# A hybrid encoder layer in fp32r: seven weight slots handed out from one free pool instead of in turn

## The chip, the cores and the metric

The kernel runs on one core of a Trainium2 chip. The metric is the device time of one launch in microseconds, the median over several runs; the profile is one further execution of the same program, recorded by the hardware profiler.

## The reference

One inference step of a layer with two branches, on a prompt of 1024 tokens and a sample of 32 tokens with a cache of 128 keys (model width 1024, 8 heads, DFF 2816). Cut to what matters:

```
mod  = silu(c) @ w_ada + b_ada                      # six shift/scale/gate vectors
h    = rms_norm(x) * (1 + scale1) + shift1
q, k, v, xin, gb, gc, ga_br, gb_br = split(h @ w_in)
o    = rms_norm(softmax(q1 k1) v - lam * softmax(q2 k2) v)   # chunk-causal, 8 heads, q/k normed
y_a  = o @ w_attn_out
y_b  = (gb * short_conv(gc * xin)) @ w_conv_out     # width 3, per channel
x    = x + gate1 * ((sigmoid(ga_br) * y_a + sigmoid(gb_br) * y_b) @ w_out)
h2   = rms_norm(x) * (1 + scale2) + shift2
g, up = split(h2 @ w_gate_up)
x    = x + gate2 * ((silu(g) * up) @ w_down)
```

## The kernel before, in words

**Precision.** Every product is computed from operands split into a high part (fp32r) and a low part (the remainder): `split` is a cast on ScalarE (L84) and a subtraction on VectorE, or on GpSimd where the caller says so (L85). Each product takes three matmuls, high times high, high times low, low times high.

**Dense stages by Strassen.** The 1056 token columns are four quarters of 264. The conv inputs (sections 3 and 5 of `w_in`), the branch gates (sections 6 and 7) and gate_up multiply a pair of 128-wide weight columns at a time: `wstrassen` loads the two columns (`kt_stage`, L108, into two staging buffers with the tag "st"), takes their four blocks A11, A12, A21, A22, forms S1 to S4 from them in place in the staging buffers (L150 S3, L152 S1, L155 S2, L160 S4) and splits seven tiles, in the order A11, A22, S2, S1, A12, S3, S4 (S4's low part on GpSimd). S2 is made from A22, S4 from A12 and S2. `strassen` multiplies in the order of `SEQ`: A11, S2, S1, A12, S3, S4, A22. Each of the seven products is 12 matmuls (L184) for each of two halves of the tokens, so a set is 168 matmuls of 264 columns. Sums and activations leave PSUM through L188 to L201; eight PSUM tiles a set come from a pool of six.

```
SEQ = (("A11", "B11", "X"), ("S2", "T2", "Y"), ("S1", "T1", "Z"), ("A12", "B21", "X"),
       ("S3", "T3", "V"), ("S4", "B22", "Z"), ("A22", "T4", "V"))
```

The conv stage has eight sets in turns (xin, then gc; after each gc set the convolution L506/L508 on VectorE), the gate stage eight sets with two `ada_step`s after each (chains of L360 on VectorE that compute the adaLN vectors, closed by small transposes on TensorE, L367), gate_up 22 sets.

**Dense stages without Strassen.** conv_out, attn_out and out split a weight column into two tiles (`wpiece`), the down projection into three for each half of DFF (`d_piece`); they use the tiles in the order in which they make them.

**Attention.** `run_plan` fixes the order of TensorE, ScalarE, VectorE and GpSimd from estimated times: 72 units (8 heads, 9 token tiles), each a generator per engine. `act_thread` writes the exponentials p (L882) into tiles of the weight slots: the planner counts five of them (`R["p"]`, a ring). `filler` computes the section gb of the projection (L1050 to L1052) wherever TensorE is free, from two further slots (`wf`, cast at L1036, low part at L1038), eight times.

**Slots.** The pool `W` holds the two staging buffers and seven weight slots of 4 KB a partition. `w_slot` gives out the tags ws0 to ws6 in turn, each with one buffer: tile number i always has the slot of tile i - 7. Also the first adaLN weights (`ada_load`) take their places so. In attention p has ws0 to ws4 in turn and `wf` ws5 and ws6. A tile's first write waits until all reads of the tile before it in its slot are done.

**Order of the work.** TensorE's instructions run in program order. Outside attention, the order of ScalarE, VectorE, GpSimd and SP (which issues the DMAs) is set by the compiler's scheduler, which takes the instruction that is first in the program among those whose operands and slots it estimates to be ready. On the chip each engine then keeps that order.

Of the kernel before, what the change touches and what calls it, by code (L numbers as in the profile page):

```python
# [7 lines left out]
F32 = mybir.dt.float32  # L8
F32R = mybir.dt.float32r
# [5 lines left out]
P = 128  # L15
D = 1024
KT = 8
# [17 lines left out]
def f(ap):  # L35
    return ap.bitcast(F32)


def hybrid_layer(tc, x_prompt, x_sample, cache_k, cache_v, state_conv, c_prompt, c_sample,
# [8 lines left out]
    def sb(name, bufs=1, side="left"):  # L48
        return tc.alloc_tile_pool(name=name, bufs=bufs, side=side, reuse_waits="tile")
# [17 lines left out]
    W = sb("W")  # L67
# [16 lines left out]
        act.copy(hi, src)  # L84
        (lo_eng or dve).tensor_sub(lo, src, f(hi))  # L85

    wsn = [0]

    def w_slot(shape, dtype, name):

        wsn[0] += 1
        return W.tile(shape, dtype, tag=f"ws{wsn[0] % 7}", name=name, bufs=1)

    def ws_tile():

# [532 lines left out]
    def run_plan():  # L628
        while threads:
# [10 lines left out]
            try:  # L640
# [5 lines left out]
    R = {k: Ring(n) for k, n in (("qd", 4), ("kraw", 3), ("kd", 3), ("QK", 2), ("p", 5), ("aT0", 2), ("aT1", 1), ("o", 2),  # L646
                                 ("on", 2), ("sq", 1), ("cv", 2))}
# [22 lines left out]
    def head_tiles(h):  # L670
        if h not in heads:
            K = A.tile([P, 8, 2, P], F32R, tag="K", name="K", bufs=2)
            Ks = A.tile([P, 2, P + DS], F32R, tag="Ks", name="Ks", bufs=2)
            V = A.tile([P, 10, VD], F32, tag="V", name="V", bufs=2)
            ck = A.tile([P, 2, HD], F32, tag="ck", name="ck", bufs=1)
            sp.dma_start(ck, cache_k[0, 0, :, h])
            sp.dma_start(V[:, 8, :], cache_v[0, 0, :, h])
            heads[h] = K, Ks, V, ck
        return heads[h]
# [147 lines left out]
    def act_thread(k):  # L827
        h, t = divmod(k, 9)
        u, n = units[k], (P if t < 8 else DS)
        K, Ks, V, ck = head_tiles(h)  # L830
        if t < 8:
            src = lambda: u["pj_t"]
            ev, vdst = u["pj"], V[:, t, :]
            v_out = v_prompt[0, 0, t * P:(t + 1) * P, h]
        else:
            e = yield "ACT", 0.47, [u["pj"]]
            s0 = u["s0_t"] = A.tile([DS, 384], F32, tag="s0", name="s0", bufs=1)
            act.copy(s0, u["pj_t"][DS:2 * DS, 0:384])
            u["s0"].t = e.t
            src = lambda: s0  # L840
            ev, vdst = u["s1"], V[:DS, 9, :]
            v_out = v_sample[0, 0, :, h]
        e = yield "ACT", 0.42, [ev, R["sq"]]
        u["sq_rel"] = R["sq"].take()
        sq = u["sq_t"] = A.tile([P, 256], F32, tag="sq", name="sq", bufs=1)
        act.activation(sq[:n], src()[:n, 0:256], AF.Square, scale=0.125)
        u["sq"].t = e.t
        e = yield "ACT", 0.28, [R["kraw"]]
        u["kraw_rel"] = R["kraw"].take()
        kraw = u["kraw_t"] = A.tile([P, 2 * HD], F32, tag="kraw", name="kraw", bufs=3)  # L850
        act.copy(kraw[:n], src()[:n, 128:256])
        u["kraw"].t = e.t
        e = yield "ACT", 0.38, [R["qd"]]
        u["qd_rel"] = R["qd"].take()
        qd = u["qd_t"] = A.tile([P, 2, 2, HD], F32, tag="qd", name="qd", bufs=4)
        act.copy(qd[:n], src()[:n, 0:128].rearrange("p (m d) -> p m d", m=2).unsqueeze(2).to_broadcast([n, 2, 2, HD]))
        u["qd"].t = e.t
        e = yield "ACT", 0.29, []
        act.copy(vdst, src()[:n, 256:384])
        sp.dma_start(v_out, vdst)  # L860
        u["V"].t = e.t
        if t < 8:
            u["pj_rel"].t = e.t
        if t == 8:
            e = yield "ACT", 0.48, [u["Kc"]]
            act.activation(Ks[:, :, 0:P], u["ck_p"][:, 0:2, :], AF.Copy, scale=gq)
            u["ckh"].t = e.t
        kdst = K[:, t] if t < 8 else Ks[:, :, P:P + DS]
        e = yield "ACT", 0.37, [u["tr"]]
        act.copy(u["QH_t"][:, :, :n], u["tr_t"][:, 0:2, :n])  # L870
        u["QH"].t = e.t
        e = yield "ACT", 0.48, []
        act.activation(kdst, u["tr_t"][:, 2:4, :n], AF.Copy, scale=gq)
        u["K"].t = e.t
        sums = u["sums"] = A.tile([P, 2], F32, tag="sums", name="sums", bufs=9)
        u["p_t"], u["p_rel"] = [], []
        for m in range(2):
            L = lambda: u["L"]
            e = yield "ACT", 0.62 + (0.0008 * 128 * min(t + 1, 8) if t < 8 else 0.1), [u[f"n{m}"], R["p"]]
            u[f"p{m}_rel"] = R["p"].take()  # L880
            p = W.tile([P, 1024], F32, tag=f"ws{len(R['p'].rel) % 5}", name="p", bufs=1)
            act.activation(p[:n, :u["L"]], u["sv"][m][:n], AF.Exp, bias=u["nmx"][:n, m:m + 1],  # L882
                           scale=u["rs_t"][:n, m:m + 1], accum_out=sums[:n, m:m + 1])
            u["p_t"].append(p)
            u[f"e{m}"].t = e.t
            if not u["both"] or m == 1:
                u["S_rel0" if u["both"] else f"S_rel{m}"].t = e.t
        e = yield "ACT", 0.59 if t > 2 else 0.4, [u["tA0"], R["aT0"]]
        u["aT_buf"] = [R["aT0"].take()]
        aT_evict(u, 0, n)  # L890
        u["a0"].t = u["aT_rel"][0].t = e.t
        e = yield "ACT", 0.37, [u["av"], R["o"]]
        u["o_rel"] = R["o"].take()
        o = u["o_t"] = A.tile([P, VD], F32, tag="o", name="o", bufs=2)
        act.activation(o[:n], u["av_t"][:n, :VD], AF.Copy, scale=u["r_t"][:n, 0:1])
        u["o"].t = u["av_rel"].t = e.t
        e = yield "ACT", 0.5, []
        junk = A.tile([P, VD], F32, tag="junk", name="junk", bufs=1)
        rn = u["rn_t"] = A.tile([P, 1], F32, tag="rn", name="rn", bufs=9)
        act.activation(junk[:n], o[:n], AF.Square, accum_out=rn[:n])  # L900
        u["jk"].t = e.t
        e = yield "ACT", 0.37, [u["tO"]]
        ot = A.tile([P, P], F32, tag="ot", name="ot", bufs=2)
        act.activation(ot[:, :n], u["ot_p"][:, :n], AF.Copy, scale=gsub)
        sp.dma_start(oT_d[h, :, t * P:t * P + n] if t < 8 else oT_d[h, :, S:T], ot[:, :n])
        u["ot"].t = u["ot_rel"].t = e.t

    def aT_evict(u, x, n):
        pt, bs = u["aT_p"][x]
        aT = A.tile([P, 4, P], F32, tag=f"aT{x}", name="aT", bufs=2 - x)  # L910
        u["aT_t"].append(aT)
        vb = u["vb"]
        runs = [(0, len(bs), P)] if all(vb[b][1] == P for b in bs) else [(b - bs[0], b - bs[0] + 1, vb[b][1]) for b in bs]
        for i0, i1, w in runs:
            (dve.tensor_copy if x else act.copy)(aT[:w, i0:i1, :n], pt[:w, i0:i1, :n])
# [111 lines left out]
    def filler():  # L1027

        read = Ev(0.0)
        for n in range(KT):  # L1030
            e = yield "ACT", 0.05, [stages]
            rel = stages.take()
            v = kt_stage(win_v[:, :, (4 * KT + n) * P:(4 * KT + n + 1) * P])
            e = yield "ACT", 1.05, [Ev(e.t + 4.0), read]
            wh, wl = (W.tile([P, KT, P], F32R, tag=f"ws{i}", name="wf", bufs=1) for i in (5, 6))
            act.copy(wh, v)  # L1036
            e = yield "DVE", 1.22, [e]
            dve.tensor_sub(wl, v, f(wh))  # L1038
            rel.t = e.t
            for g0, gw in GROUPS:  # L1040
                pt = None
                cv = A.tile([P, GW], F32, tag="cv", name="cv", bufs=2)
                sp.dma_start(cv[:, :gw], cv_d[n, :, g0:g0 + gw])
                for kt in range(KT):
                    e = yield "PE", 0.483, [e, Ev(8.0) if kt else Ev(30.0), h_ready[kt]] + ([banks] if pt is None else [])
                    if pt is None:
                        i, rel = banks.take()
                        pt = bank(i)
                    ah, al = hA[kt][:, 0, g0:g0 + gw], hA[kt][:, 1, g0:g0 + gw]
                    pe.matmul(pt[:, :gw], wh[:, kt, :], ah, start=kt == 0, stop=False)  # L1050
                    pe.matmul(pt[:, :gw], wh[:, kt, :], al, start=False, stop=False)
                    pe.matmul(pt[:, :gw], wl[:, kt, :], ah, start=False, stop=kt == KT - 1)  # L1052
                read = e
                d = yield "DVE", 0.48, [e]
                dve.tensor_mul(cv[:, :gw], pt[:, :gw], cv[:, :gw])
                sp.dma_start(z_d[n, :, g0:g0 + gw], cv[:, :gw])
                rel.t = d.t
# [474 lines left out]
```

## Time and profile before

| | |
|---|---|
| median of 3 runs | 2237.26 us (2235.27 to 2238.21) |
| profiled execution | 2239.61 us |
| its span, first to last instruction | 2237.8 us |
| mean granted TensorE clock | 0.968 |
| TensorE busy (matmuls) | 2076.3 us, 93% of the span |
| VectorE busy | 1363.7 us, 61% |
| ScalarE busy | 851.9 us, 38% |
| GpSimd busy | 358.2 us, 16% |

A line of the profile names the engine (PE and PEld TensorE's matmuls and weight loads, DVE VectorE, ACT ScalarE, POOL GpSimd, SPq the DMA queue of SyncE), the line of the kernel, the operation, the tile written and those read. In a row in order of time the first number is the start in us from the beginning of the span, the second the duration; "x24" counts instructions merged in the row, and a bracket gives the engine's idle time just before and what ended it. In a row of waits the numbers are the total in us, the number of times and the longest. A stretch of the busy-time view is given with the busy time of each engine, its instructions, the granted clock as a share of full speed, and the DMA engines' share.

### The profile page before, as it was taken

The numbers are of one execution on the slowest core, as the hardware profiler recorded it, in microseconds if no ns is written. First come the engines' busy times: TensorE is split into PE (matmuls) and PEld (weight loads), VectorE is DVE, ScalarE is ACT, GpSimd is POOL, SyncE is SP. The second block draws the span as 40 slices with busy tenths as digits, with TensorE's granted clock in tenths as the row PEclk, the third lists the DMA queues.
The fourth block names the chain that finished last, engine by engine and source line by source line (L and its number), as shares of the span: only waits on it lengthen the run. The fifth ranks groups of instructions, "written<-read, shape, count | busy, mean of one in ns | idle before, by whom it ended". The sixth has DMA issues, their size and how long they took to land. (4 is left out here: it accounts for less than half of the span.)

```text
span 2237.8 us, 37742 instructions
## 1 busy us (share of the span) xinstructions
PE 2076.3 (93%) x14339; PEld 2004.4 (90%) x14339; DVE 1363.7 (61%) x3096; ACT 851.9 (38%) x2044; POOL 358.2 (16%) x660
## 2 busy tenths in 40 slices
PE   6888888879999999999989998979999999999999
PEld 5788888879999998899889998979999999999998
DVE  4866667776677767766546885585555555542332
ACT  5522232236666666666422212363232232321210
POOL 1012200003333333333200000001111211100000
PEclk9899999989999999999999999989999999999999
DMA  8421133352122111211278643223312222362321
GB/s 261 134 68 57 58 114 116 116 162 84 56 69 67 53 51 55 71 51 54 66 222 266 202 135 108 82 68 99 94 58 81 79 70 77 101 208 70 102 72 55
DMA packets 298960, 224.41 MB, mean 100 GB/s; under 512 B 15618, under 2 KB 281499, under 8 KB 298779
## 3 DMA queue, kind: packets, MB, share of 16 engines
q1 hardware_dynamic: 298778, 222.00, 32.5%
q8 instruction: 113, 1.85, 0.3%
q14 instruction: 69, 0.56, 0.1%
HBM read 162.46 MB, written 59.49 MB: 99 GB/s over the span
## 5 line engine op out<-in xcount | busy, mean ns | idle before, releaser
L84 ACT CAST ws<-st 128x512 fp32r<-128x512 f32 x360 | 218.7, 615 | 664.2 <-PE u L184 164.7
L184 PE MATMUL u<-op,ws 128*128 128x264 f32 x3168 | 409.6, 287 | 19.3 <-ACT op L84 6.5
L184 PEld LDWEIGHTS u<-op,ws 128*128 128x128 f32 x3168 | 395.9, 189 | 28.6 <-DVE ws L85 10.7
L85 DVE TENSOR_TENSOR ws<-st,ws 128x512 fp32r<-128x512 f32 (+1 forms) x322 | 228.7, 715 | 165.7 <-ACT ws L84 164.7
L184 PE MATMUL u<-T,ws 128*128 128x264 f32 x1536 | 222.2, 305 | 53.9 <-ACT ws L84 51.6
L184 PEld LDWEIGHTS u<-T,ws 128*128 128x128 f32 x1536 | 212.4, 207 | 60.2 <-ACT ws L84 54.6
L734 PE MATMUL b<-qw,hA 128*128 128x384 f32 x512 | 186.5, 364 | 2.5 <-DVE adred L369 1.3
L735 PE MATMUL b<-qw,hA 128*128 128x384 f32 x512 | 174.0, 340 | 1.3 <-DVE qw L691 1.3
L736 PE MATMUL b<-qw,hA 128*128 128x384 f32 x512 | 173.6, 339 | 0.0
L1434 PE MATMUL u<-ka,ws 128*128 128x352 f32 x480 | 157.3, 328 | 2.2 <-ACT ka L84 2.2
L1436 PE MATMUL u<-ka,ws 128*128 128x352 f32 x480 | 156.2, 325 | 3.1 <-DVE ws L85 3.1
L1435 PE MATMUL u<-ka,ws 128*128 128x352 f32 x480 | 156.1, 325 | 1.4 <-DVE ka L85 1.4
L184 PE MATMUL u<-B,ws 128*128 128x264 f32 x1152 | 151.9, 287 | 4.2 <-ACT B L84 4.2
L184 PEld LDWEIGHTS u<-B,ws 128*128 128x128 f32 x1152 | 145.7, 190 | 4.8 <-ACT B L84 4.5
L85 POOL TENSOR_TENSOR ws<-st,ws 128x512 fp32r<-128x512 f32 x38 | 50.1, 1318 | 577.5 <-ACT ws L84 577.5
L360 DVE SCALAR_TENSOR_TENSOR adacc<-adw,sc,adacc 128x128 f32<-128x128 f32 x448 | 137.7, 358 | 1.0
L882 ACT ACTIVATE p<-S,nmx,rs 128x128 f32<-128x128 f32 (+5 forms) x144 | 113.1, 787 | 50.3 <-DVE nmx L962 16.6
L734 PEld LDWEIGHTS b<-qw,hA 128*128 128x128 f32 x512 | 97.4, 190 | 6.4 <-issue 2.1
L735 PEld LDWEIGHTS b<-qw,hA 128*128 128x128 f32 x512 | 97.6, 191 | 1.9 <-DVE qw L691 1.6
L736 PEld LDWEIGHTS b<-qw,hA 128*128 128x128 f32 x512 | 97.0, 189 | 0.0
L1436 PEld LDWEIGHTS u<-ka,ws 128*128 128x128 f32 x480 | 91.0, 190 | 3.4 <-DVE ws L85 3.4
L1434 PEld LDWEIGHTS u<-ka,ws 128*128 128x128 f32 x480 | 91.2, 190 | 2.5 <-ACT ka L84 2.5
(277 smaller groups left out, 4378.8 us busy)
## 6 DMA issues: line engine op xcount, KB each, us to landing
adw<-in_w_ada_dram SPq DMA_DIRECT2D x48, 512.0 KB, 4.0
st<-in_w_gate_up_dram SPq DMA_DIRECT2D x44, 512.0 KB, 4.3
st<-in_w_in_dram SPq DMA_DIRECT2D x43, 512.0 KB, 4.2
sa<-a_d SPq DMA_DIRECT2D x22, 528.0 KB, 3.8
a_d<-xa SPq DMA_DIRECT2D x84, 132.0 KB, 1.7
st<-in_w_in_dram SPq DMA_DIRECT2D x42, 256.0 KB, 2.9
st<-in_w_down_dram SPq DMA_DIRECT2D x16, 512.0 KB, 4.8
h_d<-xnT SPq DMA_DIRECT2D x8, 528.0 KB, 4.4
```

Of the source, the lines that this page charges most:

```text
L84: act.copy(hi, src)
L85: (lo_eng or dve).tensor_sub(lo, src, f(hi))
L184: pe.matmul(q[dst], l, t[:, r, j, :], start=first and j == n == 0, stop=j == 3 and n == 2, skip_group_check=not first)
L360: dve.scalar_tensor_tensor(out=acc[:, s_, :], in0=st[:, kt, :], scalar=sc[:, 8 * s_ + kt:8 * s_ + kt + 1], in1=acc[:, s_, :], op0=ALU.mult ...
L734: pe.matmul(pj[:, 0:384], a, qh[:, :, c, :], start=kt == 0, stop=False)
L735: pe.matmul(pj[:, 0:384], a, ql[:, :, c, :], start=False, stop=False)
L736: pe.matmul(pj[:, 0:384], b, qh[:, :, c, :], start=False, stop=kt == KT - 1)
L882: act.activation(p[:n, :u["L"]], u["sv"][m][:n], AF.Exp, bias=u["nmx"][:n, m:m + 1], scale=u["rs_t"][:n, m:m + 1], accum_out=sums[:n, m:m ...
L1434: pe.matmul(pt[:, :gw], wh, ah, start=kt == 0, stop=False)
L1435: pe.matmul(pt[:, :gw], wh, al, start=False, stop=False)
L1436: pe.matmul(pt[:, :gw], wl, ah, start=False, stop=kt == KC - 1)
```

## The change

All seven slots get one tag with seven buffers, so that a tile takes any slot that is free at its turn, and the slot it waits for, if any, is one that the scheduler gave it. p and `wf` take their tiles from the same pool; the planner's own rings and the order that it writes are as before.

```
-    wsn = [0]
-
     def w_slot(shape, dtype, name):
-        wsn[0] += 1
-        return W.tile(shape, dtype, tag=f"ws{wsn[0] % 7}", name=name, bufs=1)
+        return W.tile(shape, dtype, tag="ws", name=name, bufs=7)
...
-            p = W.tile([P, 1024], F32, tag=f"ws{len(R['p'].rel) % 5}", name="p", bufs=1)
+            p = w_slot([P, 1024], F32, "p")
...
-            wh, wl = (W.tile([P, KT, P], F32R, tag=f"ws{i}", name="wf", bufs=1) for i in (5, 6))
+            wh, wl = (w_slot([P, KT, P], F32R, "wf") for _ in range(2))
```

## The prediction

> **What bounds the kernel now.** I read the page's busy shares first, then the busy time by stage, then who waited for whom, then the order of time around one typical wait of each stage.
>
> ```profile
> span 2237.8 us, 37742 instructions
> PE 2076.3 (93%) x14339; PEld 2004.4 (90%) x14339; DVE 1363.7 (61%) x3096; ACT 851.9 (38%) x2044; POOL 358.2 (16%) x660
> PEld u L184 <- ACT ws L84: 63.9, 34, 7.8
> PEld u L184 <- DVE ws L85: 16.4, 36, 2.1
> ACT ws L84 <- PE u L184: 164.7, 82, 5.5
> ```
>
> TensorE is the bound, busy in 93% of the span. The waits (total, times, longest) say what its weight loads lack: in L184, the Strassen matmuls, they stood 63.9 us for a cast of a weight tile and 16.4 us for its low part, 80.3 us in all. The third row closes the circle: those casts themselves waited 164.7 us for L184. A weight tile waits for a slot, and the slot for the set of products before.
>
> The busy time by stage (columns as in its head; the stages are conv, gates, the last gate set with the loads for attention, attention with its filler, gate_up):
>
> ```profile
> core 0: us, PE busy (x) PEld busy (x) DVE busy (x) ACT busy (x) POOL busy (x), PEclk, DMA share, GB/s
> 104.00:309.85 205.85, 178.88 (x1347) 175.49 (x1347) 131.61 (x262) 46.34 (x89) 41.12 (x68) 0.92 0.23 73
> 309.85:473.30 163.45, 136.48 (x1032) 133.80 (x1032) 123.92 (x343) 48.36 (x104) 8.24 (x6) 0.95 0.37 118
> 473.30:500.80 27.50, 20.17 (x149) 19.37 (x148) 22.51 (x57) 11.57 (x20) 1.42 (x1) 0.87 0.63 197
> 500.80:1143.00 642.20, 620.04 (x3939) 586.39 (x3940) 432.46 (x1084) 386.76 (x1163) 211.54 (x464) 0.99 0.22 65
> 1507.40:1936.70 429.30, 420.49 (x3354) 412.51 (x3355) 233.71 (x421) 128.99 (x262) 71.42 (x80) 1.00 0.26 79
> ```
>
> A set has 168 matmuls, so these are 8 conv sets (25.7 us each), 6 gate sets (27.2 us) and 20 gate_up sets (21.5 us). One gate transition, in order of time:
>
> ```profile
> 363.41 1.97 SPq L110 DMA_DIRECT2D st<-in_w_in_dram  x2
> 367.99 0.62 ACT L84 CAST ws<-st 128x512 fp32r<-128x512 f32 x1 [4.49 <-DMA st<-in_w_in_dram]
> 371.04 0.69 DVE L150 TENSOR_TENSOR st<-st 128x512 f32<-128x512 f32 x1 [1.48 <-DMA st<-in_w_in_dram]
> 382.55 0.62 ACT L84 CAST ws<-st 128x512 fp32r<-128x512 f32 x1 [0.58 <-PE u L184]
> 382.70 3.19 PE L184 MATMUL u<-B,ws 128*128 128x264 f32 x24
> 384.01 3.23 DVE L360 SCALAR_TENSOR_TENSOR adacc<-adw,sc,adacc 128x128 f32<-128x128 f32 x12
> 387.88 0.68 DVE L85 TENSOR_TENSOR ws<-st,ws 128x512 fp32r<-128x512 f32 x1
> 388.68 0.68 DVE L155 TENSOR_TENSOR st<-st 128x512 f32<-128x512 f32 x1
> 389.45 0.62 ACT L84 CAST ws<-st 128x512 fp32r<-128x512 f32 x1 [3.09 <-DVE st L155]
> 390.12 0.51 PE L184 MATMUL u<-T,ws 128*128 128x264 f32 x2 [4.23 <-ACT ws L84]
> 390.88 7.29 PE L184 MATMUL u<-T,ws 128*128 128x264 f32 x46 [0.25 <-DVE ws L85]
> 391.01 1.42 POOL L85 TENSOR_TENSOR ws<-st,ws 128x512 fp32r<-128x512 f32 x1 [26.02 <-ACT ws L84]
> ```
>
> The first of the two raw loads has landed by 367.99 (A11's cast), the second, which holds A21 and A22, by 371.04. The cast at 382.55, released by the end of L184's set, is A22 of the next set: seven tiles a set, seven slots in turn, so each tile always has the slot of its namesake. A22 is made second but multiplied last, so the new A22 waits for the whole old set. S2 is made from A22 in place (L155) and multiplied second. Behind the late cast DVE has queued an adaLN chain (L360), and only then come A22's low part (387.88), S2 (388.68) and its cast (389.45). TensorE has A11's 24 matmuls as cover, then stands 4.23 us.
>
> **The change part by part.**
>
> *The dense sets: the order of the slots.* No instruction is added or removed, nothing moves between engines; a cast may take any slot that is free. I assume that the slot free longest is given out first. In a set the slots come free in the order of multiplication: A11, S2, S1, A12, S3, S4, A22. The next set's tiles ask in the order in which they are made: A11, A22, S2, S1, A12, S3, S4. So A22 gets S2's old slot after two products instead of seven, S2 gets S1's after three, and S4, the last, gets A22's at the end. S4's low part is then ready a cast and a GpSimd subtraction later (0.62 + 1.42 = 2.0 us), and is multiplied sixth, five products in. Everything else has more room. On SP, a load of the next raw weights now waits for S4 at a set's end; the adaLN loads and the stores queued behind it wait along, none of them asked for within the next 2 us. The second raw load goes out once S4 is split, so some 2 us into the next set, and lands 4.6 us after issue (363.41 to 367.99): 6.6 us into that set. A22, which it brings, can have a slot from 5.9 us on (48 of the matmuls costed below) and is used a set later. The waits of TensorE on weights should go. What is late next is looked for below, by stage.
>
> The cadence of an unhindered set, and the small gap of gate_up, are in these rows:
>
> ```profile
> 1507.38 1.78 SPq L110 DMA_DIRECT2D st<-in_w_gate_up_dram  x2
> 1525.15 0.62 ACT L84 CAST ws<-st 128x512 fp32r<-128x512 f32 x1 [5.26 <-PE u L184]
> 1528.46 0.51 PE L184 MATMUL u<-op,ws 128*128 128x264 f32 x2 [0.47 <-ACT ws L84]
> 1529.18 13.02 PEld L184 LDWEIGHTS u<-op,ws 128*128 128x128 f32 x106 [0.43 <-DVE ws L85]
> 1916.81 1.75 SPq L110 DMA_DIRECT2D st<-in_w_gate_up_dram  x2
> ```
>
> 106 weight loads in 13.02 us are 0.1228 us each, 20.63 us a set. From 1507.38 to 1916.81 are 19 sets at 21.55 us: each loses 0.92 us.
>
> - gate_up: 3354 matmuls at 0.1228 are 411.9 us of 429.30, so at best -17.4. DVE is at 54%, nothing else is near. I take 20.75 us a set (0.12 left for semaphores), 20 sets 415.0: **-14.3**. At worst half of the best is gained, L85 or a raw load being late at times: -8.7.
> - conv: 1347 x 0.1228 = 165.4 of 205.85, at best -40.4. DVE is at 131.61, 16.5 a set: room, but unevenly spread, which the next rows show. I take 20.63 + 0.8, about the loss that gate_up has today, 21.4 a set, 171.2: **-34.7**. At worst half the best: -20.
>
> ```profile
> 174.50 0.62 ACT L84 CAST ws<-st 128x512 fp32r<-128x512 f32 x1 [5.26 <-PE u L184]
> 175.68 2.43 POOL L477 TENSOR_TENSOR u<-t,sg 128x264 f32<-128x264 f32 x2 [1.01 <-DVE t L200]
> 178.95 2.73 DVE L508 SCALAR_TENSOR_TENSOR z<-u,vec,z 128x528 f32<-128x528 f32 x4
> 181.60 0.68 DVE L155 TENSOR_TENSOR st<-st 128x512 f32<-128x512 f32 x1
> 182.98 9.05 PE L184 MATMUL u<-T,ws 128*128 128x264 f32 x48 [5.64 <-ACT ws L84]
> ```
>
> Here the convolution (L508) stands between A22's cast and S2. After the change S2 is made in the set before; L508 then delays only the additions that empty PSUM; of its six banks a set needs again the first only at the fifth product, 4 x 24 x 0.1228 = 11.8 us in. On GpSimd S4's subtraction can stand behind the gating products (L477, 2.43 us), which leaves 14.7 - 2.0 - 2.4 = 10 us before its use, five products in.
>
> - gates: 1032 x 0.1228 = 126.7 of 163.45, at best -36.8, 21.1 a set. But DVE has 123.92 us of work there, 20.65 a set: TensorE and DVE would run neck and neck, and DVE's queue has a fixed order, so it will lose something to waits. I take 22.6 a set, a quarter of today's loss of 6.1 kept, 135.6: **-27.9**. At worst half kept: -18.
>
> The clock is in these sums. After the 4.23 us gap 46 matmuls took 7.29 us against 46 x 0.1228 = 5.65, 1.64 lost; after the 5.64 us gap 48 took 9.05 against 5.89, 3.16 lost. With four such gaps in conv and six in gates: 4 x 3.16 + 6 x 1.64 = 22.5 of the 77.2 at best there.
>
> [...]
>
> *The last gate set.*
>
> ```profile
> PE pad L367 <- DVE adacc L360: 6.1, 2, 5.4
> ```
>
> At the end of the gates TensorE waits 5.4 us for DVE's last adaLN chain. The cold start of this set (1.64) goes; if DVE is the later one, the wait grows as much. I take **0**, ends -1.6 and +5.4.
>
> *Attention: p and the filler's weights.* Both keep their order, written by the planner. Five slots for p in turn and two for wf become seven for both.
>
> ```profile
> ACT wf L1036 <- PE b L1051: 21.0, 2, 14.7
> PE b L1050 <- ACT wf L1036: 3.3, 3, 1.3
> PE b L1052 <- DVE wf L1038: 1.6, 3, 0.7
> ACT p L882 <- DVE nmx L962: 16.6, 20, 2.3
> ```
>
> The exponentials (L882) wait for the maximum, not for p's slot, so p gains nothing. The filler's cast stood for its own old slot twice, when the units had run out and five p slots lay idle; TensorE lost 3.3 + 1.6 = 4.9 us on wf. I take **-3** for those two, ends -4.9 and 0 (a loss is a rival).
>
> *The other dense stages* (conv_out, attn_out, out, down) take tiles in the order in which they use them; a free pool then hands out the same slots. Nothing.
>
> **Sum.** -14.3 - 34.7 - 27.9 + 0 - 3 = -79.9 us. The profiled execution took 2239.6 us (span 2237.8), so 2159.7; the median shown is 2.35 lower, so 2157.4. Best ends: -17.4 - 40.4 - 36.8 - 1.6 - 4.9 = -101.1, 2136. Worst ends: -8.7 - 20 - 18 + 5.4 + 0 = -41.3, 2196.
>
> **The rivals.**
>
> *DVE takes over.* In the gates and after each convolution DVE has its fixed order; each wait on a cast or on PSUM there is TensorE's. For it: 20.65 us of DVE work against 21.1. Against: 12 us and more of room for each weight. If the gates gain nothing and conv half: -14.3 - 20 - 3 = -37, 2200.
>
> *The slot was not the cause.* If the cast at 382.55 came late because of its place in ACT's order, nothing changes: 2237. Against: it starts 0.15 us before the next set's matmuls, 1525.15 does the same in every gate_up set, and the raw data lay there for 11.5 us (371.04).
>
> *Slower: attention's exponentials inherit the filler's slots.* Up to 16 times (8 blocks, two tiles) a p could get a slot that the filler's matmuls still read; the cast or exponential then waits in ACT's queue and all behind it. The two such waits today are 14.7 and 6.3 us. At 6.3 us each 16 cost 100.8 us: with the dense gain of 76.9 that is 2261. It decides from 13 of them on, if all reach TensorE. Against: TensorE is busy 620 of 642 us, it runs ahead by several units, and p's and wf's together still hold at most seven.
>
> [...]
>
> **How the numbers follow.** My forecast, 2136 to 2185: 0.62. DVE takes over, 2185 to 2230: 0.25. No change: 0.05. Slower: 0.08. The likeliest case gives 2157. Range 2134 to 2204: it reaches over some two thirds of the second case and leaves out the rest of it and the last two. A difference of 0.2%, 4.5 us, is about what can be told from no change. Faster 0.87, same 0.05, slower 0.08.
>
> **What would show it.** The casts of A22 start two products after the set begins; L184's weight loads wait under 15 us for ws; the conv and gate stages have a granted clock of 0.98 or more; a gate_up set takes 20.6 to 20.9 us, a conv set under 21.8, a gate set 21.1 to 23.5 with DVE over 88% busy; wf's cast waits for no matmul in the tail. Wrong if the L184 waits stay but name a DMA or a DVE addition, or if the attention stretch grows past its 642 us.

## The result, and the profile after

| | before | after |
|---|---|---|
| median of four runs each, us | 2236.28 | 2134.11 |
| lowest to highest, us | 2235.27 to 2238.21 | 2131.08 to 2137.38 |
| ratio | 1 | 0.9542, 95% interval 0.9526 to 0.9559 |
| profiled execution, us (span) | 2239.6 (2237.8) | 2132.99 (2131.2) |

The change makes the kernel 4.6% faster, 102 us where 80 were forecast. The lines of the changed kernel from the slots on stand three lower than before: the Strassen matmuls are L181, the adaLN chain L357, attention's first matmuls L731. First the busy shares of the page of after, then rows of its waits (total, times, longest):

```profile
span 2131.2 us, 37806 instructions
PE 2031.0 (95%) x14339; PEld 1976.7 (93%) x14339; DVE 1351.4 (63%) x3096; ACT 847.1 (40%) x2044; POOL 364.7 (17%) x660
```

```profile
PE u L181 <- ACT op L84: 6.5, 1, 6.5
PE pad L364 <- DVE adacc L357: 17.2, 5, 7.4
ACT ws L84 <- PE u L181: 172.9, 91, 6.4
```

TensorE's waits on ws in the Strassen matmuls (80.3 us of weight loads before) are gone from the list: what is left there are waits on operands. ScalarE still waits 172.9 us for L181, more than before. That is the lesson of this row: casts wait for slots as ever, but nobody waits for them.

The same stages before and after, each from the first copy of a product (L188, now L185) to a later one or to a stage's first matmul. Columns: from:to, length, busy time of PE, PEld, DVE, ACT, POOL, granted clock, DMA share, GB/s. The stages are conv (8 sets), gates (6), the last gate set and the loads, attention, conv_out, gate_up (20 sets), its last set. First before:

```profile
101.75:307.98 206.23, 179.10 (x1350) 175.50 (x1349) 131.99 (x263) 46.53 (x88) 41.12 (x68) 0.92 0.23 71
307.98:466.67 158.69, 136.03 (x1035) 133.60 (x1034) 119.16 (x326) 48.01 (x103) 8.24 (x6) 0.95 0.37 118
466.67:500.90 34.23, 22.34 (x163) 21.10 (x161) 29.14 (x78) 13.60 (x23) 1.42 (x1) 0.88 0.59 187
500.90:1143.90 643.00, 620.89 (x3945) 587.22 (x3946) 432.50 (x1084) 386.66 (x1162) 211.54 (x464) 0.99 0.22 65
1143.90:1246.30 102.40, 97.57 (x588) 94.92 (x586) 67.72 (x162) 27.66 (x35) 0.00 (x0) 0.98 0.88 271
1505.35:1936.04 430.69, 421.67 (x3363) 413.37 (x3362) 235.06 (x423) 129.95 (x263) 71.42 (x80) 1.00 0.26 79
1936.04:1959.30 23.26, 20.78 (x156) 20.35 (x155) 14.86 (x22) 8.16 (x12) 4.67 (x5) 0.93 0.55 163
```

And after:

```profile
101.36:269.79 168.43, 166.27 (x1356) 165.64 (x1355) 135.51 (x270) 45.05 (x90) 43.98 (x69) 1.00 0.28 87
269.79:397.20 127.41, 127.41 (x1046) 127.41 (x1045) 119.07 (x331) 47.21 (x105) 9.06 (x7) 1.00 0.49 154
397.20:424.80 27.60, 18.23 (x142) 17.26 (x142) 24.20 (x70) 11.02 (x20) 0.00 (x0) 0.86 0.61 198
424.80:1067.70 642.90, 621.26 (x3944) 588.19 (x3945) 433.85 (x1087) 389.19 (x1165) 211.24 (x464) 0.99 0.23 66
1067.70:1166.40 98.70, 95.33 (x589) 93.49 (x587) 60.35 (x146) 23.08 (x28) 0.00 (x0) 1.00 0.85 259
1422.76:1834.09 411.33, 411.33 (x3363) 411.33 (x3362) 227.79 (x424) 130.39 (x263) 76.19 (x81) 1.00 0.28 84
1834.09:1852.90 18.81, 18.81 (x156) 18.81 (x155) 11.80 (x20) 7.19 (x11) 4.82 (x6) 1.00 0.59 174
```

By stage: conv -37.8, gates -31.3, last gate set -6.6, attention -0.1, conv_out -3.7, gate_up -19.4 and its last set -4.4, down (278.5 to 278.3) -0.2. The stages not shown give -3.1 together. The spans differ by 106.6 where the medians differ by 102.2, because the profiled execution of before lies above its median and that of after below. In the gates and in gate_up TensorE is busy for the whole stretch at full clock: nothing is left there to gain from slots. One gate set of after, in order of time (some rows left out):

```profile
332.25 0.28 DVE L354 TENSOR_SCALAR adacc<-adw,sc 128x128 f32<-128x128 f32 x1
...
337.61 0.62 ACT L84 CAST ws<-st 128x512 fp32r<-128x512 f32 x1 [3.41 <-DMA st<-in_w_in_dram]
...
343.56 0.68 DVE L85 TENSOR_TENSOR ws<-st,ws 128x512 fp32r<-128x512 f32 x1
344.27 0.69 DVE L152 TENSOR_TENSOR st<-st 128x512 f32<-128x512 f32 x1
...
344.99 0.62 ACT L84 CAST ws<-st 128x512 fp32r<-128x512 f32 x1 [2.54 <-DVE st L152]
...
351.02 2.69 PE L181 MATMUL u<-B,ws 128*128 128x264 f32 x20
351.55 1.39 DVE L354 TENSOR_SCALAR adacc<-adw,sc 128x128 f32<-128x128 f32 x1
351.56 1.29 POOL L85 TENSOR_TENSOR ws<-st,ws 128x512 fp32r<-128x512 f32 x1 [19.71 <-ACT ws L84]
```

A22's cast, at 337.61, now waits for its raw data and no longer for a product; its low part follows at 343.56, S2 is made at 344.27 and cast at 344.99, all six microseconds and more before the next set begins at 351.02. Before, the cast began 0.15 us ahead of that beginning, and all the rest came behind it. S4's low part (351.56) is the only thing left behind the end of a set, as the prediction had it.

### The profile page after: what moved, and what is told of

Its sections match the earlier page's. It is cut to its first block, busy times and chain, and to the rows that moved or that the text cites. A ratio compares the mean times of both kernels' runs of the same rounds, so it can differ in the third digit from the quotient of the medians.

```text
span 2131.2 us, 37806 instructions
## 1 busy us (share of the span) xinstructions
PE 2031.0 (95%) x14339; PEld 1976.7 (93%) x14339; DVE 1351.4 (63%) x3096; ACT 847.1 (40%) x2044; POOL 364.7 (17%) x660
## 5 line engine op out<-in xcount | busy, mean ns | idle before, releaser
L84 ACT CAST ws<-st 128x512 fp32r<-128x512 f32 x360 | 217.2, 615 | 564.4 <-PE u L181 172.9
L181 PE MATMUL u<-op,ws 128*128 128x264 f32 x3168 | 397.3, 285 | 7.8 <-ACT op L84 6.5
L181 PEld LDWEIGHTS u<-op,ws 128*128 128x128 f32 x3168 | 392.4, 189 | 8.4 <-ACT op L84 6.7
L85 DVE TENSOR_TENSOR ws<-st,ws 128x512 fp32r<-128x512 f32 (+1 forms) x322 | 222.6, 699 | 195.3 <-ACT ws L84 192.9
L181 PE MATMUL u<-T,ws 128*128 128x264 f32 x1536 | 198.5, 287 | 1.2 <-DVE sg L197 1.2
L181 PEld LDWEIGHTS u<-T,ws 128*128 128x128 f32 x1536 | 193.5, 190 | 1.8 <-DVE sg L197 1.8
L731 PE MATMUL b<-qw,hA 128*128 128x384 f32 x512 | 186.8, 365 | 2.5 <-DVE adred L366 1.2
L181 PE MATMUL u<-B,ws 128*128 128x264 f32 x1152 | 152.1, 287 | 4.6 <-ACT B L84 4.6
L181 PEld LDWEIGHTS u<-B,ws 128*128 128x128 f32 x1152 | 145.6, 190 | 5.3 <-ACT B L84 4.9
L357 DVE SCALAR_TENSOR_TENSOR adacc<-adw,sc,adacc 128x128 f32<-128x128 f32 x448 | 132.8, 350 | 0.6
L731 PEld LDWEIGHTS b<-qw,hA 128*128 128x128 f32 x512 | 97.7, 191 | 6.4 <-issue 2.1
```

The source lines that it names most:

```text
L181: pe.matmul(q[dst], l, t[:, r, j, :], start=first and j == n == 0, stop=j == 3 and n == 2, skip_group_check=not first)
L357: dve.scalar_tensor_tensor(out=acc[:, s_, :], in0=st[:, kt, :], scalar=sc[:, 8 * s_ + kt:8 * s_ + kt + 1], in1=acc[:, s_, :], op0=ALU.mult ...
L731: pe.matmul(pj[:, 0:384], a, qh[:, :, c, :], start=kt == 0, stop=False)
```

## The experiments

Each kernel was timed beside the kernel before on the same chip; on one chip, with `order_alone`, `one_product_earlier`, `attention_in_turn` and `changed_again`, its median was 2241.86 us, on another, with the other four, 2240.64 us. So the ratio is the number to compare.

**The order of release without a pool.** The kernel before, with this edit alone:

```
+   handed = dict(A11=0, A22=1, S2=2, S1=3, A12=4, S3=5, S4=6)
    ...
+       old = dict(handed)
+       handed.update(A11=old["A11"], A22=old["S2"], S2=old["S1"], S1=old["A12"], A12=old["S3"], S3=old["S4"],
+                     S4=old["A22"])
-           w[o] = ws_tile()
+           w[o] = W.tile([P, 2, 4, P], F32R, tag=f"ws{handed[o]}", name="ws", bufs=1)
```

> The kernel before, all slots in turn as before, but the seven slots of a set are handed on by a fixed list in the order in which the multiplication leaves them: A22 gets S2's old slot, S2 gets S1's, S1 A12's, A12 S3's, S3 S4's, S4 A22's. Theory 'order': what the pool gave in the dense stages is only that A22 no longer waits for the last product. Then conv takes 20.6 us a set, gates 21.0, gate_up 20.6 as in the changed kernel, and only what the pool gave outside the Strassen sets is missing (3.7 us in conv_out, 0.1 in attention): about 2138 us. Rival 'freedom': the pool counts because any late tile can take any slot; then sets still stand for weights, the clock in conv or gates stays below 0.98, and the time is 2150 us or more.

Measured: 2156.93 us, ratio 0.9619 (0.9599 to 0.9639). The stages conv, gates, gate_up with its last set, down:

```profile
101.70:269.40 167.70, 166.38 (x1358) 165.84 (x1357) 135.61 (x273) 45.24 (x89) 43.14 (x69) 1.00 0.28 87
269.40:396.00 126.60, 126.60 (x1040) 126.60 (x1039) 117.78 (x328) 48.05 (x105) 9.04 (x7) 1.00 0.49 154
1440.20:1870.40 430.20, 430.20 (x3517) 430.20 (x3517) 236.39 (x439) 135.42 (x270) 80.55 (x86) 1.00 0.28 86
1870.40:2156.00 285.60, 270.40 (x1658) 266.57 (x1656) 84.15 (x137) 48.47 (x70) 0.81 (x2) 0.98 0.32 101
```

Inside the Strassen stages the theory holds: 167.7, 126.6 and 430.2 us against 168.4, 127.4 and 430.1 (411.33 + 18.81) with the pool, all at a clock of 1.00. The total is 19 us above that theory's nevertheless, and so among the totals of the rival; but the rival's signs, sets that stand for weights and a clock under 0.98 in conv or gates, are absent. conv_out took 102.4 us, as foreseen; most of the rest lies in places that neither account had named: the entry of gate_up (from the first matmul with the second norm's factors to the second set 85.9 us, 11.4 more than with the pool) and down (7.3 more). There a stage that takes slots in plain turn and a Strassen stage, which takes them by the list, meet. At the entry of gate_up TensorE stood 8.0 us for the cast of one weight tile (1403.39). The casts ahead of it had waited for the matmuls of out, the first until 1388.13, 3.7 us later in the stretch than with the pool. That the slots handed to them were the reason is argued, not shown.

**The same order, with the seams closed.** The slots as one ring, in every dense stage; a Strassen set puts them back in the order of multiplication:

```
+       ring.append(ring.pop(0))
+       return W.tile(shape, dtype, tag=f"ws{ring[-1]}", name=name, bufs=1)
        ...
+       made = dict(zip(("A11", "A22", "S2", "S1", "A12", "S3", "S4"), ring))
+       ring[:] = [made[o] for o, _, _ in SEQ]
```

> The kernel before; its seven slots are still fixed when the program is written, but kept as one ring in the order in which they come free, in all dense stages: a Strassen set takes the ring in the order in which its tiles are made and puts it back in the order in which they are multiplied, every other stage takes and puts back in the order of use. Attention keeps its five and two slots in turn. The run with the fixed hand-over inside Strassen alone lost 3.7 us in conv_out, 11 at the entry of gate_up and 7 in down, where the stage before left the slots in another order than the plain turn asks for them. Theory 'order of release is all': these seams close too, the dense stages are those of the changed kernel, and the time is that of the changed kernel with attention in turn, 0.954 of before (2134 to 2139 us). Rival 'a pool decides at run time': the seams stay, 0.962 (2157 us).

Measured: 2139.62 us, ratio 0.9551 (0.9528 to 0.9573), which overlaps the changed kernel's 0.9526 to 0.9559. Two of the three seams closed: the entry of gate_up (the same stretch) took 74.7 us against 74.5 with the pool and 85.9 in the first experiment, and conv_out 97.7 (first row). Gate_up with its last set took 430.24. In the second row, down did not follow:

```profile
1068.80:1166.50 97.70, 94.69 (x587) 93.43 (x586) 60.25 (x146) 23.07 (x28) 0.00 (x0) 1.00 0.84 262
1853.60:2138.00 284.40, 270.23 (x1657) 267.06 (x1656) 82.35 (x134) 46.84 (x67) 0.88 (x2) 0.98 0.31 98
```

So the gain is the order in which slots are passed on, at two stage changes too, and a list fixed in advance gives all of it but some microseconds in down. Down took 6.1 us more than after and 4.1 more than in the second profile of the changed kernel (280.3 us). Of the 6.1, 2.2 are idle time of TensorE, a wait of 2.7 us for a low part among it, and 3.9 are matmuls that lasted longer, at a granted clock of 0.98 against 0.99. Why stays open, and whether a free choice is worth something there too.

**One product instead of five.** The kernel before; A22 and S4 swap their slots in each set, `handed.update(A22=handed["S4"], S4=handed["A22"])`, so A22 waits for six products where it waited for seven.

> The kernel before, with one edit: in each set A22 and S4 swap their slots, so that A22 waits for six products instead of seven, 24 matmuls or 2.95 us less. Theory 'order, with the clock on top': the gates' gap of 4.23 us falls to about 1.3 and the 1.64 us of slow clock behind it go as well, so a gate set falls from 27.3 to about 22.7 us; a long conv set from 31.2 to about 25.1 (5.64 us gap to 2.7, and 3.16 us of clock), the short one to 20.6; gate_up, which lost 0.92, to 20.6. Sum -23 - 27 - 19 = -69: about 2167 us. Rival 'gap alone': the clock is slow for another reason (the load of the engines), then only 2.95 us go from each long gap and the granted clock stays at 0.92 and 0.95: 8 x 1.8 + 6 x 2.95 + 19 = -51, 2185 us. Rival 'place in the queue': A22's cast stands where it does for another reason and nothing moves: 2236 us.

Measured: 2186.47 us, ratio 0.9753 (0.9732 to 0.9774), close to the second account's total, but by another sum. Conv and gates, conv's waits, and one conv set:

```profile
104.05:300.10 196.05, 174.56 (x1347) 172.57 (x1346) 133.47 (x266) 47.23 (x90) 45.74 (x69) 0.94 0.24 74
300.10:426.50 126.40, 126.40 (x1037) 126.40 (x1037) 115.15 (x322) 47.92 (x103) 8.29 (x7) 1.00 0.47 148
```

```profile
PE u L187 <- DVE ws L85: 14.3, 4, 3.6
```

```profile
177.90 2.73 DVE L511 SCALAR_TENSOR_TENSOR z<-u,vec,z 128x528 f32<-128x528 f32 x4
180.55 0.68 DVE L85 TENSOR_TENSOR ws<-st,ws 128x512 fp32r<-128x512 f32 x1
181.29 8.62 PE L187 MATMUL u<-T,ws 128*128 128x264 f32 x46 [3.62 <-DVE ws L85]
```

The gates are cured altogether (126.4 us, clock 1.00): there the earlier cast lets S2 slip in ahead of the adaLN chain. In one gate set S2 is made at 338.73, while the last product runs, and the chain's first operation comes at 341.56. Conv gained only 10.2 of its 37.8 us: there S2 itself now comes earlier, but its low part (180.55) still stands behind the convolution (L511), and TensorE waits for it. So the worth of a slot that comes 2.95 us earlier is not in proportion to these 2.95 us. What counts is on which side of DVE's next long run the weight's steps fall. None of the three accounts had that. The entry of gate_up and down are longer than before here too (9 and 5 us), as the seams of the first experiment were; attention is 7.5 us longer, for no settled reason.

**Attention in turn.** The changed kernel; attention holds seven tiles, p takes five of them in turn, `f(att[len(R['p'].rel) % 5])`, and the filler's weights the other two.

> The changed kernel, with one part of it undone: in attention and conv_out seven tiles are held, five for p in turn and two for the filler's weights in turn, as before the change; the dense stages keep the pool. Theory: the pool is worth nothing inside attention (the late low part behind a multiplication took what the two waits gave), and 3.7 us at conv_out, whose weights found free p slots: stages before attention as in the changed kernel, attention 643 us, conv_out 102.4 instead of 98.7, 2138 us in all. Rival, the prediction's term: attention itself also loses 3 us, 2141. Rival: none of it belongs to the pool, 2134.

Measured: 2138.85 us, ratio 0.9542 (0.9523 to 0.9560). The changed kernel once more, on the same chip:

> The changed kernel once more, to be compared with the other kernels on the same chip: 2134 us.

Measured: 2133.57 us, ratio 0.9523 (0.9503 to 0.9542). Attention and conv_out with the slots held in turn; the changed kernel's second profile has 642.9 and 97.3 us for them:

```profile
423.70:1069.50 645.80, 623.38 (x3944) 589.04 (x3945) 434.34 (x1087) 388.44 (x1165) 210.48 (x464) 0.99 0.23 66
1069.50:1165.90 96.40, 93.81 (x583) 92.89 (x582) 57.67 (x137) 23.08 (x28) 0.00 (x0) 1.00 0.84 257
```

The total is the first account's, but not its sum. Attention is 2.9 us longer in turn, what the rival gave, but its waits don't show it: TensorE stands 3.3 + 1.6 = 4.9 us for the filler's weights in turn, and 4.8 with the pool, by rows further down. The totals differ by 0.2%, with intervals that overlap. So attention's own share is between nothing and 3 us, and which is not settled. The 102.4 us expected of conv_out were wrong: its weights still come from the pool, and the casts of its second pair of tiles waited only for their load (1053.94). The ring above, a fixed list that hands out p's five slots first, had conv_out at 97.7 us as well. That is once more order, not freedom.

**More work for DVE in the gates.** Two kernels, the changed one with overwritten operations at the head of each adaLN chain; the first has the first of these two lines once per chain, the second has both twice:

```
+            dve.tensor_scalar(out=acc[:, i % 2, :], in0=st[:, i, :], scalar1=sc[:, 0:1], scalar2=None, op0=ALU.mult)
+            dve.scalar_tensor_tensor(out=acc[:, i % 2, :], in0=st[:, i, :], scalar=sc[:, i:i + 1], in1=acc[:, i % 2, :], ...
```

> The changed kernel with more work for DVE in the gates: each adaLN chain begins with one more TENSOR_SCALAR on 128x128, whose result is overwritten. By the row of that form (0.516 us) and two chains a set, DVE's work goes from 19.85 to 20.88 us a set, beside 21.0 of TensorE. Theory 'the larger sum decides, whatever the order': the set stays at 21.0 us, only the last chain's wait grows by about 1 us: 2135 us. Rival, the prediction's term: neck and neck, a fixed order costs TensorE part of a set before the sums meet, 1.5 us a set: gate sets of 22 us or more, 2143 us.

> The changed kernel with two more TENSOR_SCALAR and two more SCALAR_TENSOR_TENSOR on 128x128 in each adaLN chain of the gates (overwritten): 2 x 2 x (0.516 + 0.343) = 3.4 us a set, so DVE's work is 23.3 us against 21.0 of TensorE. Theory 'the larger sum decides': gate sets of 23.3 us, DVE 99% busy, TensorE's gaps short enough for the clock to stay above 0.95: 6 x 2.3 + about 3 at the last chain = 17 us, 2151 us. Rival, the prediction's: waits and slow clock come on top, 25 us a set and more, clock below 0.95: 2161 us or more.

Measured: 2135.26 us, ratio 0.9531 (0.9510 to 0.9552), and 2144.10 us, ratio 0.9567 (0.9541 to 0.9594). In the lighter one the gates took 127.33 us with 120.86 us of DVE work, no longer than in the changed kernel. An early and a late gate set of the heavier one:

```profile
293.01:314.01 21.00, 21.00 (x175) 21.00 (x174) 20.65 (x61) 7.69 (x17) 1.31 (x1) 1.00 0.37 111
356.21:378.18 21.97, 21.84 (x177) 21.42 (x176) 21.52 (x65) 7.60 (x18) 1.64 (x2) 1.00 0.48 147
```

The added work was smaller than forecast: the mean of 0.516 us for a TENSOR_SCALAR holds ones that are stretched beside GpSimd, 1.39 us at 351.55 above against 0.28 at 332.25. But the question is answered. At 20.65 us of DVE work in 21.00 (98%) TensorE loses nothing; at 21.5 the set is 22.0 (the next one 21.9), the clock stays at 1.00. The larger sum decides to within half a microsecond: the 1.5 us a set of the prediction are not there, and what there is, some 0.4 us, comes only once DVE's sum is the larger one.

**A version from these readings.** After the change, TensorE's longest waits for DVE that could be moved are the pad transposes of the adaLN chains (17.2 us, quoted above). The chains of the last gate set and of the last unit of attn_out go to gate_up, where DVE has room:

```
+            if (sec, p) != (7, KT - 2):
+                ada_step()
+                ada_step()
...
+        st = w_slot([P, KT, P], F32, "adw") if late[0] else sbp.tile([P, KT, P], F32, tag="adw", name="adw", bufs=2)
...
+        if f0 == 0:
+            B, late[0] = sb("Bd"), 1
+        if ada_todo or ada_open:
+            ada_step()
```

> A version meant to be faster: the changed kernel, with the adaLN chains of the last gate set and of the last unit of attn_out left out there and done in gate_up, where DVE is at 55%; their weights are loaded into slots of the pool. Nothing of the computation is left out. In the changed kernel TensorE waits 17.2 us in all for these chains at its pad transposes, 7.4 of them at the end of the gates, and starts attention with a slow clock. Theory: most of that goes, 12 to 17 us: about 0.948 of before, 2119 us. Rival 'the next late thing takes over' (the loads for attention's operands and the additions behind them): 5 us or less, 2130 us. Rival 'a fifth customer of the pool': the long-lived adaLN weights keep a slot for a whole chain and a set waits for it again: slower than 2134 us.

Measured: 2123.06 us, ratio 0.9475 (0.9455 to 0.9496), below the 0.9542 and 0.9523 of the changed kernel by 0.5 to 0.7%, and outside their intervals. The rows are the end of the gates and the gate_up sets with chains:

```profile
398.72:418.80 20.08, 17.43 (x143) 17.21 (x142) 14.37 (x34) 8.53 (x18) 0.00 (x0) 1.00 0.59 191
1409.80:1641.60 231.80, 229.42 (x1861) 227.81 (x1861) 148.46 (x326) 67.44 (x143) 50.30 (x48) 1.00 0.33 99
```

The end of the gates falls from 27.6 to 20.1 us, the stretch from attn_out to the second norm's factors from 181.9 to 170.2. Attention (647.2 us) gives 4.3 back, and the 11 sets with chains are 231.8 us where 11 x 20.57 would be 226.3. Of these 5.5 us, 2.4 are idle time of TensorE, and its waits there name no weight: they are 2.1 us for additions of DVE that empty PSUM (L197). So the third account, a slot held too long, is not what shows; the chains in DVE's order fit better, and the rest stays open. It beats both kernels, by less than hoped.

## Why the prediction was right, and where not

- **The mechanism: right.** A22's slot is free in time (its cast, 7.6 us into the set where two products take 5.9, waits only for its load), S4's low part comes last, no wait for ws is left in the Strassen matmuls, the clock is 1.00 in conv and gates, and a set of gate_up takes 20.57 us (411.33 / 20) against the 20.6 to 20.9 named. Order alone gave the same Strassen stages, so the reason is the order, as argued, and not the free choice.
- **The size: wrong.** The time came out 23 us below the forecast, at the low edge of its range and past the best end of its sum, 2136 us. What failed is the sizing of the terms, and the first four were all too small. Of the profiled spans' 106.6 us the sum had 79.9; the 26.7 missing are 10.0 in the gates with their last set, 9.5 in gate_up, 7.0 in stages put at nothing and 3.1 in conv, less 2.9 in attention, the fifth, which was sized too large. Some 3 us of this are a misread row: 13.02 us of 106 weight loads hold 105 steps and one whole load (189 ns by the page), so the cadence is not 0.1228 us but 0.1223 (411.33 us / 3363 matmuls after), and the best ends were not the best.
- *Gates, "a quarter of today's loss of 6.1 kept" because TensorE and DVE "would run neck and neck".* -27.9 forecast, with 0 for the last gate set; measured -31.3 and -6.6, -37.9 together against -38.4 at the best ends. No loss was kept: 119.07 us of DVE work in 127.41 us cost nothing, and in the heavier kernel 98% cost nothing either. The margin for friction was taken from no row, and the one row that bore on it had DVE's work (20.65 us a set) below TensorE's (21.1). The rival "DVE takes over" falls with it.
- *Conv, "20.63 + 0.8, about the loss that gate_up has today".* -34.7 forecast, -37.8 measured (168.43 / 8 = 21.05 a set). Gate_up's loss came from the same late slot that the change removes; it should not have been carried over.
- *Gate_up, 0.12 a set left for semaphores and the last set forgotten.* -14.3 forecast; -19.4 for 20 sets and -4.4 for the last. Nothing was left for semaphores. The stretch priced, of 3354 matmuls, ended with the set before the last; in the last one of before, S2's low part (1938.60) stood behind the split of an operand for down, took 1.75 us where it takes 0.68 elsewhere, beside a GpSimd subtraction (1938.51, 1.30 us), and S2 itself had been made late because of A22's late cast:

```profile
1938.60 1.75 DVE L85 TENSOR_TENSOR ws<-st,ws 128x512 fp32r<-128x512 f32 x1
1940.40 3.01 PE L184 MATMUL u<-op,ws 128*128 128x264 f32 x12 [1.93 <-DVE ws L85]
```

- *"The other dense stages ... Nothing."* Measured 3.7 in conv_out and, with the stretches not listed, 3.1 more. Within a stage the free pool does hand out the same slots; between two stages it does not. Before, the casts of conv_out's second pair of weight tiles, next in turn for a slot of the filler, waited for its matmuls until conv_out itself began (1143.9), and the cast of the next z operand came 2.8 us behind, waiting for its load. After, these weights had found free slots at 1060.13, 7.6 us ahead of conv_out's beginning (1067.7), and the cast of the z operand came 1.6 us ahead of it. That the late casts kept the raw tile into which z had to be loaded fits this order, but was not tried by itself. First before, then after:

```profile
1143.90 1.14 ACT L84 CAST ws<-st 128x512 fp32r<-128x512 f32 x2 [2.15 <-PE b L1051]
1146.65 1.07 ACT L84 CAST z<-st 128x1056 fp32r<-128x1056 f32 x1 [1.61 <-DMA st<-z_d]
```

```profile
1060.13 1.14 ACT L84 CAST ws<-st 128x512 fp32r<-128x512 f32 x2 [12.15 <-DMA st<-in_w_conv_out_dram]
1066.10 1.08 ACT L84 CAST z<-st 128x1056 fp32r<-128x1056 f32 x1 [0.50 <-DMA st<-z_d]
```

- *Attention, -3.* Measured -0.1. The two casts did lose their waits (they follow each other at 1026), but the low part made from the second now stands behind a multiplication in DVE's order, and TensorE waits for that instead:

```profile
1041.37 0.53 DVE L1052 TENSOR_TENSOR cv<-b,cv 128x352 f32<-128x352 f32 x1 [3.35 <-PE b L1049]
1041.81 1.21 DVE L1035 TENSOR_TENSOR wf<-st,wf 128x1024 fp32r<-128x1024 f32 x1
1043.08 0.42 PE L1049 MATMUL b<-hA,wf 128*128 128x352 f32 x1 [1.42 <-DVE wf L1035]
```

```profile
PE b L1049 <- DVE wf L1035: 3.5, 3, 1.4
PE b L1047 <- ACT wf L1033: 1.3, 1, 1.3
```

  These 4.8 us stand against the 4.9 of before. The slower rival, exponentials behind the filler's slots, did not occur: attention did not grow.
- **The clock: right.** Conv went from 0.92 to 1.00 and the gates from 0.95 to 1.00, as forecast. The 22.5 us of slow clock stood in the best ends, and these were nearly reached; no run isolates them. The figure took one gap of each stage for all and measured from 5.65 and 5.89 us, while such matmuls at full clock last 5.90 (46) and 6.04 (48). By the rows of all ten gaps it is about 20.6, 11.4 in conv and 9.3 in the gates. Nor does the length of a gap alone decide what it costs: see the last section.
- **The last gate set, "0, ends -1.6 and +5.4".** The wait for the adaLN chain did grow, from 5.4 to 7.4 us; but the last of the long gaps fell into this stretch when it is cut at the products, so that it gained 6.6.

## What to carry to other kernels

When tiles are made in one order and used in another, slots handed on in turn make a tile wait for its namesake; hand them on in the order in which they come free, by a pool or by a fixed list, and look at the seams between stages as well. Price a tile that comes earlier by which side of the next long run of the fixed-order engine it lands on, not by the microseconds it gains. Where the best end of a term is bounded by rows, take friction off it only if a row shows friction: an engine whose work stays below the bound's own time cost nothing here, up to 98%.

## What the runs showed of the hardware

The length of a gap alone does not price the slow clock behind it. At full clock (1.00) 46 matmuls in a row last 5.90 us (104.03 before) and 48 last 6.04 (333.04 after). Before, in conv, 48 took 8.85 us at a granted clock of 0.67 behind a gap of 7.62 us (132.24), 8.62 at 0.69 behind one of 7.13 (235.13), 9.05 at 0.66 behind one of 5.64 (182.98) and 9.02 at 0.66 behind one of 5.06 (285.45), so the longer gaps cost less, 2.81 and 2.58 us against 3.01 and 2.98. In the kernel of the third experiment 46 took 8.62 us (181.29) behind a gap of 3.62 us, with one of 1.35 and two matmuls ahead of it: 2.72 us lost. In the gates of before 46 took 7.29 us at 0.79 (390.88) behind a gap of 4.23 us, two matmuls and 0.25 us: 1.39 lost. What decides beside the length, no run here shows.

A TENSOR_SCALAR of 128x128 took 1.39 us beside a GpSimd subtraction of 1.29 us that began 0.01 us after it (351.55 after), 1.02 us beside one that had begun 0.36 us before it (341.56, third experiment), and 0.28 us with none beside it (332.25 after). Both of the long ones ended 0.09 us after the subtraction; a mean over such a group prices neither kind. One that began 0.06 us ahead of a subtraction took 0.28 us all the same (372.55 after). What holds some of them back, no run here shows.
